# Residual gates of a two-layer diffusion backbone: rows spread over the partitions through a scratch in DRAM in place of a shuffle and GpSimd broadcasts

## The chip, the cores and the metric

The kernel runs on one core of one Trainium2 chip. The metric is the device time of one execution in microseconds, taken as the median of several runs. The core has five engines that run at the same time and meet through semaphores: TensorE (PE in the profile, with its weight loads as PEld), VectorE (DVE), ScalarE (ACT), GpSimd (POOL) and SyncE (SP). SP computes nothing here. It issues every DMA of this program, one after another, and stops at an instruction whose semaphore has not yet come, with all later DMAs behind it.

## The reference

One inference step of a transformer-like trunk: 2 layers over 128 context tokens and 256 latent tokens, 1024 features. The two groups share the weights and differ in the modulation, which is computed from a conditioning vector of each:

```
for l in range(DEPTH):
    sh1, sc1, g1, sh2, sc2, g2 = split(silu(c) @ w_mod[l] + b_mod[l], 6)
    h  = rmsnorm(x, norm1_g) * (1 + sc1) + sh1
    p  = h @ w_in                       # recurrence heads, attention heads
    o_r = gated linear recurrence, both directions (4 heads)
    o_a = attention with normalised q and k, rotary for latent tokens (8 heads)
    x  = x + g1 * (concat(o_r, o_a) @ w_out)
    h2 = rmsnorm(x, norm2_g) * (1 + sc2) + sh2
    x  = x + g2 * (relu(h2 @ w1) ** 2 @ w2)
y = rmsnorm(x, final_norm_g)
```

g1 and g2 are the residual gates. Each is a row of 1024 numbers for the context tokens and another for the latent tokens; all tokens of a group use the same row. The change touches only how these rows get to where the update of x reads them.

## The kernel before, in words

**Tiles.** The 384 tokens are three tiles of 128 tokens: tile 0 is the context, tiles 1 and 2 the latent tokens. `x[t]` holds 128 tokens on the partitions and 1024 features. Every product is made in three parts: each operand is split into a high part that TensorE takes at full rate (`hi`, made by an ACT cast, line 356) and the rest (`lo`, made by a DVE subtraction, line 364), and high by high, low by high and high by low are summed in PSUM.

**Weights.** All weights stream in from DRAM as units of up to 128 x 1024 numbers (512 KB), issued on SP by `load_chain` (line 348). A unit lands in one of four `raw` tiles. It leaves that tile when DVE has made its `lo` part, or, for the units of the modulation `w_mod` that are summed on DVE (`mod_acc`, lines 378 and 380), when DVE has made its four products with the two conditioning vectors. So SP mostly waits for a `raw` tile, and a load starts when DVE frees one. `hi` and `lo` have four tiles each, and parts of larger regions take more units in the MLP.

**The gates.** There are four: (layer 0, g1), (layer 0, g2), (layer 1, g1), (layer 1, g2), in the code `(l, ("g", 0))` and `(l, ("g", 1))`. The products of `w_mod` with the conditioning leave a gate in a PSUM bank as 4 x 256 numbers on partitions 0, 32, 64, 96 for the context and on partitions 1, 33, 65, 97 for the latent tokens. `mod_chain` then adds the bias on DVE (`brow`, line 442, into a `gev` tile), copies the latent rows from partitions 1, 33, ... to 0, 32, ... with a DVE shuffle (line 444), and spreads each of the eight pieces over all 128 partitions of `G` with eight GpSimd broadcasts (line 448). `G` is one tile of 128 x 2 x 1024 for all four gates, so a gate can be written only when the gate before it has been used up; the key `gfree` says so. The third gate waits for that at the end of layer 0.

**The update of x.** For each token tile and each half of the features, `xupd_chain` multiplies the PSUM bank of the products by `G` on DVE (line 638) and adds the result to x, the first half on POOL and the second on DVE (line 641).

**The norm.** `rms_steps` sums the squares of a tile on ACT (line 473), adds the two halves on DVE (line 475) and raises the sum to the power -1/2 on POOL (line 476, one column of 128 numbers). DVE scales x by that (line 487), TensorE transposes the scaled tile in eight pieces (line 492), ACT and DVE apply the modulation (lines 506, 504), and they split the result into `Hh` and `Hl` (lines 515, 516), which the next products read. The powers for the q, k and recurrence norms are made on POOL too (line 467).

**The end of a layer.** After the last products with w2 (line 1148) the three tiles get their update and their norm for the next layer one after the other, and the products with the q, k and v columns of w_in follow (`qk_part`, lines 568 and 569: six products for a unit of weights and a token tile; the first four units are taken for the tiles 0, 1 and 2 in turn, then the last four).

**The order of the work.** Nothing is left to the hardware: a class `Sched` holds some hundred chains of steps, each with an engine, an assumed duration, the keys it reads and writes and the tiles it takes and frees. It plays a rough model of the engines, and emits the step that could start first, with priorities; each engine then runs its list in order. A change of the assumed engine or duration of a step therefore moves other steps too.

Of the kernel before, what the change touches and what calls it, by code (L numbers as in the profile page):

```python
# [4 lines left out]
F32 = mybir.dt.float32  # L5
# [8 lines left out]
L = 2  # L14
# [11 lines left out]
class Sched:  # L26
    """Emits the steps of several chains in the order in which a rough model of the engines could start them."""

# [87 lines left out]
def c_dve(n, fast=False, extra=0):  # L116
    return 0.07 + n * (0.52e-3 if fast else 1.04e-3) + 0.06 * extra
# [10 lines left out]
def step_kernel(tc, A):  # L128
# [12 lines left out]
    def sb(name, shape, dt=F32):  # L141
        return P.tile(shape, dt, name=name, tag=name)
# [34 lines left out]
    sch.add_slots("hi", [sb(f"hi{i}", [128, 1024], F32R) for i in range(4)])  # L177
    sch.add_slots("lo", [sb(f"lo{i}", [128, 1024], F32R) for i in range(4)])
    regs = {}

# [84 lines left out]
    def warm_chain(nm, since, until, cold):  # L265
        """products of zeros that keep the tensor engine's clock up while its operands are on their way"""
        z = S0[:, 0, 0:2].rearrange("p h n -> p (h n)").bitcast(BF16)
        n = 0
        while until not in sch.t:
            yield S("PE", 0.44 if n < cold else 0.22, lambda: PE.matmul(get(nm), z[:, 0:128], z[:, 0:512], start=True, stop=True), r=since, acq=[("ps", nm)] if n == 0 else [], w=[nm])  # L270
            n += 1
        if n:
            yield S("PE", 0.0, lambda: None, rel=[nm])

# [1 line left out]
    units = []  # L276
# [50 lines left out]
    def split_prio():  # L327
        # units that are ready for the products and not used yet
        left = sum(1 for k in sch.bound if k[0] == "lo")
        return 0.5 if left <= 1 else 6  # L330
# [4 lines left out]
    def early_reg():  # L335
        """before the first layer's chains need them, the regions take the weights of its modulation"""
        def f():
            rs = [regs["xnT"][:, 3072:], region("B", "eB", F32), region("C", "eC", F32)]
            sch.add_slots("raw0", [r[:, i * 1024:(i + 1) * 1024] for r in rs for i in range(r.shape[1] // 1024)])
        yield S("POOL", 0.0, f, acq=[("rB", "eBr"), ("rC", "eCr")], r=["xnTreg"], w=["early"])  # L340
        yield S("POOL", 0.0, lambda: None, r=[("modps", 0, tag) for tag in mod_tags(0)[0]], rel=["eBr", "eCr"], w=["early_done"])
# [24 lines left out]

# [1 line left out]
    def mod_acc(l, tag):  # L368
# [15 lines left out]
    def mod_chain(l, tag):  # L384
# [7 lines left out]
        if (l, tag) in mod_dve:  # L392
            # the products with the two conditioning vectors on DVE, the sum over partitions on PE
            acc = {(i, h): ("modacc", l, tag, i, h) for i in range(2) for h in range(2)}

            def mm():
                for i in range(2):
                    for j in range(4):
                        m = 32 if i == 0 else 2
                        PE.matmul(get(nm)[32 * j:32 * j + m, 0:256], sel[:, 32 * i:32 * i + m], get(acc[i, j // 2])[:, (j % 2) * 256:(j % 2) * 256 + 256], start=i == 0, stop=i == 1, tile_position=(0, 32 * j))  # L400
            yield S("PE", 1.0, mm, r=[("modacck", l, tag, i, h) for i in range(2) for h in range(2)] + ["ini"], acq=[("ps", nm)], rel=list(acc.values()) + [("mtok", l, tag)], w=[nm])
        else:
            for u in us:
                def mm(u=u):
                    raw = get(("raw",) + u)
                    for i in range(kk):
                        k = u[3] + i
                        m = 32 if k == 0 else 2
                        for j in range(J):
                            o = (i * J + j) * N  # L410
                            PE.matmul(get(nm)[32 * j:32 * j + m, 0:N], cT[:, k, 0:m], raw[:, o:o + N], start=k == 0, stop=k == 7, tile_position=(0, 32 * j))  # L411
                yield S("PE", kk * (0.51 if N == 256 else 0.29), mm, r=[("rawk",) + u, "cT"], acq=[("ps", nm)] if u is us[0] else [], rel=[("raw",) + u],
                        w=[nm] if u is us[-1] else [], key=u)
# [26 lines left out]
        else:  # L440
            gi = tag[1]
            yield S("DVE", c_dve(256), lambda: V.tensor_tensor(out=get(ev)[:, 0:256], in0=get(nm)[:, 0:256], in1=brow[:, gi, :], op=ALU.add),
                    r=[nm, ("brow", l)], acq=[("gev", ev)], rel=[nm], w=[nm + (1,)])
            yield S("DVE", c_dve(256), lambda: V.stream_shuffle(out=get(ev)[:, 256:512], in_=get(ev)[:, 0:256], mask=[1] + [0] * 31), r=[nm + (1,)], w=[nm + (2,)])
            prev = [("gfree", l, gi)] if (l, gi) != (0, 0) else []

            def pb(i, j):
                return lambda: PO.partition_broadcast(G[:, i, j * 256:(j + 1) * 256], get(ev)[32 * j:32 * j + 1, i * 256:(i + 1) * 256])
            for i in range(2):
                for j in range(4):  # L450
                    last = i == 1 and j == 3
                    yield S("POOL", 0.45, pb(i, j), r=[nm + (2,)] + prev, rel=[ev] if last else [], w=[("gate", l, gi)] if last else [])

# [6 lines left out]

# [1 line left out]
    def rstd_steps(ss, n, inv, kin, kout):  # L462
# [6 lines left out]
    def rms_steps(nm, t, xi, ss):  # L469
        """w: nm + ("rs",); returns the column with (sum x^2 + D eps)^-1/2, to be multiplied by sqrt(D) = 32"""  # L470
        for hf in range(2):
# [62 lines left out]

# [1 line left out]
    def tok_unit(l, u, k0, kk, ncol, accs, first, last, extra_r=(), acq=()):  # L536
        """activation-stationary: accs[t][:, :ncol] += h[:, t].T @ w"""
        for t in range(NT):
# [64 lines left out]
    def wout_chain(l):  # L603
        accs = {(t, hf): ("acc", l, "wo", t, hf) for t in range(NT) for hf in range(2)}

        def step(j, t, hf, last):
            """the part j of the inner dimension: first the attention's, then the recurrence's"""
            g = j if j < 4 else j - 4
# [38 lines left out]

# [1 line left out]
    def rope_prep(l):  # L649
# [28 lines left out]
    def qk_chain(l, t):  # L678
# [10 lines left out]
        yield S("DVE", c_dve(512), lambda: V.tensor_reduce(out=ss[:, 0:8], in_=v3(get(nm + ("sq",)), 8), axis=AX.X, op=ALU.add), r=[nm + ("sq",)], rel=[nm + ("sq",)], w=[nm + ("ss",)])  # L689
        # the queries' factor holds the 1/8 of the scores  # L690
        yield from rstd_steps(ss, 10, ((slice(0, 8), 1.0, 64 * EPS), (slice(8, 10), 1.0 / 64, EPS)), nm + ("ss",), nm + ("rs",))
# [44 lines left out]
        if t == 0:  # L736
            yield S("ACT", c_act(512, True), lambda: ACT.copy(out=qTs[l], in_=v3(get(pq), 4)), r=[pq, ("tokreg", l)] + prev, rel=[pq], w=[("qk", l, t)])
            return
        # a tile's queries lie where its result of the attention will: in two parts for the products with the keys
        ts = slice(t * 128, (t + 1) * 128)  # L740
# [3 lines left out]
    def attn_region(l):  # L744
        # where the recurrence will keep its products and the projections their gates
        def f():
# [94 lines left out]

# [1 line left out]
    def hg_views(l, hp):  # L843
# [12 lines left out]
    def exps(l):  # L856
        """the exponentials of a layer's attention; the sigmoids follow, so that ACT changes its tables once"""
        return [("att", l, 0, kv, "p") for kv in range(2)] + [("att", l, t, g, 2) for t in (1, 2) for g in range(4)]
# [48 lines left out]
    def hg_levels(l, hp):  # L907
        # QQ: [backward, forward]; KK, TT: [forward, backward]; units of 128 columns: 2 heads x 3 chunks
        ini = [("hgi", l, 2 * hp), ("hgi", l, 2 * hp + 1)]
        AC = ACs[hp]  # L910

        def mm(m, nm):
            QQ, KK, TT, PR = hg_views(l, hp)
            ps = get(nm)
            for u in range(6):
                o = u * 128
                if m == 64:
                    for j in range(2):
                        # rows of half j against the columns of the other half: forward from j = 0, backward from j = 1
                        PE.matmul(ps[64 * j:64 * j + 64, u * 64:u * 64 + 64], PR[:, o + 64 * j:o + 64 * j + 64], QQ[:, (1 - j) * 768 + o + (1 - j) * 64:(1 - j) * 768 + o + (1 - j) * 64 + 64],  # L920
                                  start=True, stop=True, tile_position=(0, 64 * j))
                    continue
# [154 lines left out]

# [1 line left out]
    mreg = {}  # L1079
# [32 lines left out]
    def mlp_chain(l, tail=5):  # L1112
# [14 lines left out]
        def w1_last(p):  # L1127
            """the last token tile's part of a pair of hidden tiles: tokens on the partitions, so that the products are wide"""
            a = ("zt", l, p)
# [82 lines left out]

# [1 line left out]
    def tok_reg(l):  # L1214
# [14 lines left out]

# [1 line left out]
    def mod_units(l, tag):  # L1231
# [18 lines left out]
    def mix_in(us, mods, first=0, last=None):  # L1250
        """the units of the modulation's weights, spread over the others"""
        ms = []
# [154 lines left out]
```

## Time and profile before

| | us |
|---|---|
| median of 3 runs | 1012.4 |
| lowest and highest run | 1012.01, 1016.22 |
| span of the profiled execution | 1010.4 |
| PE busy | 981.0 |
| DVE busy | 685.1 |
| ACT busy | 495.5 |
| POOL busy | 70.9 |

For the profiled execution the page gives only its span, from the first to the last instruction; a time of its own from outside is not listed. The median of the timed runs is 2.0 us above that span.

How to read the rows: in the page's groups stands the line of the kernel, the engine, the operation, what is written and read, how many times, the busy time and the mean of one. A row of the timeline has the start and the length in us, the engine, the line, the operation, and in brackets for how long the engine was idle before and what ended that. A row of the waits has who waited for whom, the total in us, how many times, and the longest. A row of the chain of waits has the start, the length and what the time belongs to. A table by windows has a stretch of the span, the busy time and number of instructions of each engine in it, then the granted clock of TensorE (1.00 is full), the share of the DMA engines and GB/s.

### The profile page before, as it was taken

To read this page: it belongs to the slowest core of one execution; us is meant where nothing else is said; L and a number is where in the kernel's file an instruction comes from. 1 tells how busy PE (TensorE), PEld (TensorE's weight loads), DVE (VectorE), ACT (ScalarE), POOL (GpSimd) and SP (SyncE) were. 2 spreads that over 40 slices of the span, in tenths; PEclk is the share of its full clock that TensorE was granted. 3 is DMA by queue.
4 is the path that set the end of the run, shared out by engine and by line. 5 is a ranking of instruction groups with operands and counts; after the bars stand their busy time and mean duration, and the time that the engine had idled before them with its cause. 6 is when DMAs were issued, how large, how long until landed. Compare 5 with 4: busy or idle time off the path is not lost.

```text
span 1010.4 us, 17391 instructions
## 1 busy us (share of the span) xinstructions
PE 981.0 (97%) x6925; PEld 837.3 (83%) x6925; DVE 685.1 (68%) x1177; ACT 495.5 (49%) x903; POOL 70.9 (7%) x81
## 2 busy tenths in 40 slices
PE   8999999999999999999996999999999999999997
PEld 5785677889988879889885988888799999999895
DVE  3687676777898888888563787987765444434434
ACT  4356655545544443434352677755555444444432
POOL 0022000111020000000021200011110000000102
PEclk9999999999999999999997999999999999999999
DMA  9957555253577777776511432242435544444411
GB/s 314 313 165 225 186 173 187 74 168 98 184 236 241 229 235 221 222 246 207 181 40 52 134 104 83 85 116 76 129 120 188 168 144 147 146 146 146 146 42 62
DMA packets 140017, 161.17 MB, mean 160 GB/s; under 512 B 5776, under 2 KB 105488, under 8 KB 139936
## 3 DMA queue, kind: packets, MB, share of 16 engines
q1 hardware_dynamic: 139936, 160.06, 51.3%
q8 instruction: 54, 0.88, 0.3%
q14 instruction: 27, 0.22, 0.1%
HBM read 157.16 MB, written 2.88 MB: 158 GB/s over the span
## 4 chain that ended last, share of the span: by engine, by line
PE 80%; DMA 10%; DVE 5%; issue 2%; ACT 1%; POOL 1%; SPq 0%; POOLq 0%; DVEq 0%; ACTq 0%
PE bank L1122 21%; PE bank L1148 21%; PE bank L587 9%; DMA raw<-w_mod_d 7%; PE bank L546 6%; PE bank L618 6%; PE bank L568 3%; DVE t L380 3%; PE bank L411 1%; PE bank L934 1%; PE bank L569 1%; PE bank L835 1%; PE bank L1137 1%; DVE lo L364 1%; PE bank L789 1%
## 5 line engine op out<-in xcount | busy, mean ns | idle before, releaser
L356 ACT CAST hi<-raw 128x1024 fp32r<-128x1024 f32 (+1 forms) x152 | 155.5, 1028 | 121.7 <-DMA raw<-w_d 42.0
L364 DVE TENSOR_TENSOR lo<-raw,hi 128x1024 fp32r<-128x1024 f32 (+1 forms) x152 | 180.5, 1195 | 43.8 <-ACT hi L356 43.3
L380 DVE SCALAR_TENSOR_TENSOR t<-raw,cT,t 128x512 f32<-128x512 f32 x196 | 135.7, 749 | 32.1 <-DMA raw<-w_mod_d 31.8
L1122 PE MATMUL bank<-mA,hi 128*128 128x384 f32 (+1 forms) x336 | 111.8, 333 | 0.0
L1122 PE MATMUL bank<-mA,lo 128*128 128x384 f32 (+1 forms) x336 | 111.1, 331 | 0.0
L1122 PE MATMUL bank<-mB,hi 128*128 128x384 f32 (+1 forms) x336 | 110.9, 330 | 0.0
L1107 ACT ACTIVATE t<-bank 128x384 f32<-128x384 f32 x64 | 31.4, 491 | 145.2 <-PE bank L1122 145.0
L1110 DVE TENSOR_TENSOR mB<-t,mA 128x384 fp32r<-128x384 f32 x64 | 35.8, 559 | 95.2 <-ACT mA L1109 95.1
L1148 PE MATMUL bank<-lo,mA 128*128 128x512 f32 x252 | 98.8, 392 | 0.0
L1148 PE MATMUL bank<-hi,mB 128*128 128x512 f32 x252 | 98.7, 392 | 0.0
L1148 PE MATMUL bank<-hi,mA 128*128 128x512 f32 x252 | 98.0, 389 | 0.0
L1122 PE MATMUL bank<-mA,wts 128*128 128x384 f32 (+1 forms) x352 | 89.0, 327 | 0.0
L1148 PE MATMUL bank<-wts,mA 128*128 128x512 f32 x264 | 87.8, 393 | 0.0
L356 ACT CAST wts<-raw 128x1024 fp32r<-128x1024 f32 x44 | 46.2, 1050 | 56.1 <-DMA raw<-w_d 28.8
L587 PE MATMUL bank<-Hh,hi 128*128 128x384 f32 x192 | 69.4, 362 | 0.6 <-ACT hg L864 0.6
L364 DVE TENSOR_TENSOR wts<-raw,wts 128x1024 fp32r<-128x1024 f32 x44 | 54.5, 1241 | 21.0 <-ACT wts L356 21.0
L1122 PEld LDWEIGHTS bank<-mA,hi 128*128 128x128 f32 x336 | 63.2, 188 | 2.6 <-issue 0.9
L587 PE MATMUL bank<-Hh,lo 128*128 128x384 f32 x192 | 64.6, 337 | 0.0
L587 PE MATMUL bank<-Hl,hi 128*128 128x384 f32 x192 | 64.5, 336 | 0.0
L1122 PEld LDWEIGHTS bank<-mB,hi 128*128 128x128 f32 x336 | 63.2, 188 | 1.3
L1122 PEld LDWEIGHTS bank<-mA,wts 128*128 128x128 f32 x352 | 62.5, 188 | 1.7 <-issue 0.9
L1122 PEld LDWEIGHTS bank<-mA,lo 128*128 128x128 f32 x336 | 63.2, 188 | 0.0
(255 smaller groups left out, 1981.3 us busy)
## 6 DMA issues: line engine op xcount, KB each, us to landing
raw<-w_d SPq DMA_DIRECT2D x128, 512.0 KB, 4.2
raw<-w_mod_d SPq DMA_DIRECT2D x80, 512.0 KB, 4.4
raw<-w_in_d SPq DMA_DIRECT2D x40, 512.0 KB, 4.9
raw<-w_in_d SPq DMA_DIRECT2D x16, 384.0 KB, 4.1
raw<-w_out_d SPq DMA_DIRECT2D x16, 256.0 KB, 4.1
raw<-w_out_d SPq DMA_DIRECT2D x8, 512.0 KB, 3.6
eB<-w_mod_d SPq DMA_DIRECT2D x12, 256.0 KB, 6.4
eC<-w_mod_d SPq DMA_DIRECT2D x8, 256.0 KB, 6.2
```

The lines of the kernel that those rows point to most:

```text
L356: yield S("ACT", c_act(n), lambda u=u, n=n: ACT.copy(out=get(("hi",) + u)[:, 0:n], in_=get(("raw",) + u)[:, 0:n]), r=[("rawk",) + u] + ([( ...
L364: yield S("DVE", c_dve(n), lambda u=u, n=n: V.tensor_tensor(out=get(("lo",) + u)[:, 0:n], in0=get(("raw",) + u)[:, 0:n], in1=get(("hi",) + ...
L380: V.scalar_tensor_tensor(out=o, in0=raw, scalar=c, in1=o, op0=ALU.mult, op1=ALU.add)
L411: PE.matmul(get(nm)[32 * j:32 * j + m, 0:N], cT[:, k, 0:m], raw[:, o:o + N], start=k == 0, stop=k == 7, tile_position=(0, 32 * j))
L546: PE.matmul(ps, a, b, start=(first and k == 0 and i == 0), stop=(last and k == kk - 1 and i == 2))
L568: PE.matmul(get(aq), a, b[:, 0:512], start=st and i == 0, stop=sp and i == 2)
L587: PE.matmul(ps, a, b, start=(k == 0 and i == 0), stop=(k == 7 and i == 2))
L618: PE.matmul(ps, a, b, start=j == 0 and i == 0, stop=j == 7 and i == 2)
L1107: yield S("ACT", c_act(384, True), lambda: ACT.activation(out=get(r_)[:, 0:384], in_=get(z)[:, 0:384], func=AF.Relu), r=[z], acq=[("t2", r ...
L1110: yield S("DVE", c_dve(384), lambda: V.tensor_tensor(out=get(u)[1], in0=get(t_)[:, 0:384], in1=get(u)[0].bitcast(F32), op=ALU.subtract), r ...
L1122: PE.matmul(get(z)[:, cs], a, b, start=(k == 0 and i == 0), stop=(k == 7 and i == 2))
L1148: PE.matmul(get(("acc", l, "w2", t, hf)), a, b, start=(f == 0 and i == 0), stop=(f == NF - 1 and i == 2))
```

## The change

The shuffle and the eight broadcasts of each gate are replaced by DMAs on SP. For each gate there is a scratch tensor in DRAM of 2 x 4 x 256 numbers. Two small DMAs write the rows of `gev` from the partitions 0, 32, 64, 96 and 1, 33, 65, 97 to it (4 x 1 KB each). A third DMA reads the 8 KB back and writes them to each of the 128 partitions of `G`, 1 MB in all. The scheduler is told that the first step takes 0.8 us and the second 3.0 us of SP. The `gev` tile is freed after the first step, and the next layer's load of `brow` (line 457), whose key is that of the removed shuffle, now follows the write to the scratch.

```diff
@@ step_kernel
+    PD = pool("dr", bass.MemoryType.DRAM)
+    gate_rows = {(l, gi): PD.tile([2, 4, 256], F32, name=f"grow{l}{gi}", tag=f"grow{l}{gi}") for l in range(L) for gi in range(2)}
...
@@ mod_chain
             gi = tag[1]
             yield S("DVE", c_dve(256), lambda: V.tensor_tensor(out=get(ev)[:, 0:256], in0=get(nm)[:, 0:256], in1=brow[:, gi, :], op=ALU.add),
                     r=[nm, ("brow", l)], acq=[("gev", ev)], rel=[nm], w=[nm + (1,)])
-            yield S("DVE", c_dve(256), lambda: V.stream_shuffle(out=get(ev)[:, 256:512], in_=get(ev)[:, 0:256], mask=[1] + [0] * 31), r=[nm + (1,)], w=[nm + (2,)])
             prev = [("gfree", l, gi)] if (l, gi) != (0, 0) else []
-
-            def pb(i, j):
-                return lambda: PO.partition_broadcast(G[:, i, j * 256:(j + 1) * 256], get(ev)[32 * j:32 * j + 1, i * 256:(i + 1) * 256])
-            for i in range(2):
-                for j in range(4):
-                    last = i == 1 and j == 3
-                    yield S("POOL", 0.45, pb(i, j), r=[nm + (2,)] + prev, rel=[ev] if last else [], w=[("gate", l, gi)] if last else [])
+            gd = gate_rows[l, gi]
+
+            def put():
+                for i in range(2):
+                    SP.dma_start(out=gd[i], in_=get(ev)[i:128:32, 0:256])
+            yield S("SP", 0.8, put, r=[nm + (1,)], rel=[ev], w=[nm + (2,)])
+            yield S("SP", 3.0, lambda: SP.dma_start(out=G.rearrange("p i n -> p (i n)"), in_=gd.rearrange("i j n -> (i j n)").partition_broadcast(128)),
+                    r=[nm + (2,)] + prev, w=[("gate", l, gi)])
```

The rest of the diff drops comments. Two lines are added near the top of `step_kernel`, so most lines of the changed kernel have a number that is 2 higher (638 becomes 640, 476 becomes 478).

The scheduler makes a new order out of this. Three places of it matter below.

**First place: the end of layer 0, on POOL.** `sm` holds the sums of squares, `pw` the exponent, the `x` tiles the three token tiles, `t` tiles are scratch. A row named ISA without operands sets up GpSimd for another kind of operation. Before:

```order
L641 TENSOR_TENSOR x_92<-x_92,t_4_111 128x512
L476 TENSOR_TENSOR sm<-sm,pw 128x1
L641 TENSOR_TENSOR x_93<-x_93,t_0_107 128x512
L476 TENSOR_TENSOR sm<-sm,pw 128x1
L641 TENSOR_TENSOR x_94<-x_94,t_0_107 128x512
L448 ISA
L448 ISA G<-gev_127 128x256 x8
L476 ISA
L476 TENSOR_TENSOR sm<-sm,pw 128x1
```

Now:

```order
L643 TENSOR_TENSOR x_92<-x_92,t_4_111 128x512
L478 TENSOR_TENSOR sm<-sm,pw 128x1
L643 TENSOR_TENSOR x_93<-x_93,t_1_108 128x512
L478 TENSOR_TENSOR sm<-sm,pw 128x1
L643 TENSOR_TENSOR x_94<-x_94,t_1_108 128x512
L478 TENSOR_TENSOR sm<-sm,pw 128x1
```

The eight broadcasts of the third gate and the two set-ups stood between the update of the third tile and the power of its norm; now the power follows the update. On the whole, POOL has no broadcast left, and no set-up but the first.

**Second place: SP at the second gate (layer 0, g2), amid the MLP weights `w_d` and the modulation `w_mod_d`.** Before:

```order
L348 DMA raw_118<-w_d 128x1024
L348 DMA raw_116<-w_mod_d 128x2x512
L457 DMA brow<-brow_d 4x512 x2
L348 DMA raw_115<-w_d 128x8x128
L348 DMA raw_117<-w_mod_d 128x2x512
```

Now:

```order
L350 DMA raw_118<-w_d 128x1024
L350 DMA raw_116<-w_mod_d 128x2x512
L451 DMA grow_130<-gev_134 4x256 x2
L350 DMA raw_115<-w_d 128x8x128
L453 DMA G<-grow_130 128x2048
L459 DMA brow<-brow_d 4x512 x2
L350 DMA raw_117<-w_mod_d 128x2x512
```

Two writes and the copy to `G` are new; the load of `brow` moves behind the copy, and the next `w_mod` unit stands behind all of them. At the first and the fourth gate it is much the same, with two and one weight loads between the writes and the copy. At the third gate the writes stand in the MLP of layer 0, and the copy far behind them, between the sixth and the seventh of the eight q, k, v units of layer 1.

**Third place: TensorE at the start of layer 1, the products of q (568, now 570) and of k and v (569, now 571) and the transposes of the third tile (492, now 494).** `hi_119` to `hi_122` are the first four units; the bank tells the token tile (before: 65 and 66 the first, 67 and 61 the second; now: 67 and 68 the first, 63 and 61 the second). Before:

```order
L568 MATMUL bank_67<-hi_120,Hl 128x512
L569 MATMUL bank_61<-hi_120,Hl 128x256
L568 MATMUL bank_67<-lo_124,Hh 128x512
L569 MATMUL bank_61<-lo_124,Hh 128x256
L492 MATMUL bank_64<-cst,t_5_112 128x128 x4
L492 MATMUL bank_68<-cst,t_2_109 128x128 x4
L568 MATMUL bank_67<-hi_121,Hh 128x512
```

Now:

```order
L570 MATMUL bank_67<-lo_126,Hh 128x512
L571 MATMUL bank_68<-lo_126,Hh 128x256
L494 MATMUL bank_65<-cst,t_0_107 128x128 x4
L494 MATMUL bank_66<-cst,t_3_110 128x128 x4
L570 MATMUL bank_63<-hi_119,Hh 128x512
```

The transposes stood behind two of the second tile's four units; now they stand ahead of all four.

## The prediction

> **What bounds the kernel now.** I read the page's totals and slices first.
>
> ```profile
> span 1010.4 us, 17391 instructions
> PE 981.0 (97%) x6925; PEld 837.3 (83%) x6925; DVE 685.1 (68%) x1177; ACT 495.5 (49%) x903; POOL 70.9 (7%) x81
> PE   8999999999999999999996999999999999999997
> GB/s 314 313 165 225 186 173 187 74 168 98 184 236 241 229 235 221 222 246 207 181 40 52 134 104 83 85 116 76 129 120 188 168 144 147 146 146 146 146 42 62
> ```
>
> TensorE is busy for 97% of the span. Taking work from DVE and POOL is worth nothing where PE never waits for it. But one slice in the middle, the 22nd (530 to 556 us), has PE at 6 tenths, and DMA is nearly silent there. So I looked for PE's longest waits, and for who made its releaser late.
>
> ```profile
> PE bank L492 <- DVE t L487: 10.3, 2, 9.8
> DVE t L487 <- POOL sm L476: 19.3, 12, 12.1
> ```
>
> One wait of 9.8 us stands out: transposes wait for DVE's scaled tile, and that waited 12.1 us for a power on POOL. The chain of waits at this place, which is the end of layer 0:
>
> ```profile
> 531.69 1.25 issue
> 532.94 3.44 POOL G L448 x8
> 536.45 6.73 issue
> 543.18 0.60 POOL sm L476
> 543.80 0.50 DVE t L487
> ```
>
> The broadcasts of the third gate are in the chain, though that gate is first read in the attention's update of layer 1, behind all its q, k, v products. The timelines of POOL and DVE tell how:
>
> ```profile
> 514.72 0.60 POOL L476 TENSOR_TENSOR sm<-sm,pw 128x1 f32<-128x1 f32 x1 [3.74 <-DVE sm L475]
> 524.78 1.94 POOL L641 TENSOR_TENSOR x<-x,t 128x512 f32<-128x512 f32 x1 [1.60 <-DVE t L638]
> 532.94 3.44 POOL L448 PARTITION_BROADCAST G<-gev  x8 [6.23 <-issue]
> 543.18 0.59 POOL L476 TENSOR_TENSOR sm<-sm,pw 128x1 f32<-128x1 f32 x1 [6.80 <-issue]
> 530.61 0.21 DVE L475 TENSOR_SCALAR sm<-sm 128x1 f32<-128x1 f32 x1
> 530.74 0.95 DVE L364 TENSOR_TENSOR lo<-raw,hi 128x768 fp32r<-128x768 f32 x1
> ```
>
> POOL ended the third tile's update at 526.72, was silent for 6.23 us, broadcast for 3.44, was silent again for 6.80, and only then made a power whose input was there at 530.82. The two silences have no releaser; they stand where POOL changes its kind of work. After the first tile, whose power follows an update directly, the same step started 0.09 us after its input (514.42 + 0.21 = 514.63, start 514.72).
>
> **What the stall costs.** TensorE around it:
>
> ```profile
> 524.43 1.04 PE L492 MATMUL bank<-cst,t 128*128 128x128 f32 x8
> 525.23 0.48 PE L1148 MATMUL bank<-wts,mA 128*128 128x512 f32 x1
> 527.38 0.39 PE L568 MATMUL bank<-hi,Hh 128*128 128x512 f32 x1
> 530.74 0.50 PE L568 MATMUL bank<-lo,Hh 128*128 128x512 f32 x1 [0.39 <-DVE lo L364]
> 544.35 1.97 PE L492 MATMUL bank<-cst,t 128*128 128x128 f32 x8 [9.81 <-DVE t L487]
> 545.97 0.78 PE L568 MATMUL bank<-hi,Hh 128*128 128x512 f32 x1
> 549.91 0.40 PE L568 MATMUL bank<-hi,Hh 128*128 128x512 f32 x1
> 550.96 0.39 PE L568 MATMUL bank<-hi,Hh 128*128 128x512 f32 x1
> 546.00:548.00 2.00, 2.00 (x8) 1.71 (x7) 1.64 (x5) 1.87 (x5) 0.00 (x0) 0.50 0.00 0
> 550.00:552.00 2.00, 2.00 (x14) 1.75 (x13) 0.32 (x1) 0.99 (x2) 0.00 (x0) 1.00 0.00 0
> ```
>
> Two terms. The wait itself is 9.81 us. And behind it the granted clock is 0.50, until the products are at 0.40 us again from 549.91 on: eight transposes take 545.97 - 544.35 = 1.62 us where the second tile's took 525.23 - 524.43 = 0.80, and two units of six products take 549.91 - 545.97 = 3.94 where one unit at full clock takes 550.96 - 549.91 = 1.05. That is 0.82 + 1.84 = 2.66 us more.
>
> Now I build the same stretch for the changed kernel, up to the same point: all products of the first two tiles with the first four units, and the third tile's transposes, are done. Before that is 549.91. After: from 527.38, four units for the first tile, 4 x 1.05 + the wait of 0.39 = 4.59, to 531.97. The transposes stand here now. The power starts 0.09 after 530.82 and takes 0.60, to 531.51; DVE ends its split at 531.69 and scales two halves of 0.44 each (0.88 for two in this trace), to 532.57. So PE waits some 0.2 us for the first half and 0.4 for the second, and has the eight transposes done at about 533.0. Four units for the second tile end at 537.2. The gain is 549.91 - 537.2 = **12.7 us**. The third tile's Hh and Hl follow the transposes as before, by 537, covered by the second tile's 4.2 us. Everything after, to the end of the span, hangs on TensorE, busy nearly without a gap, and moves forward with it.
>
> Of the clock: after 9.81 us without work the next product of 512 columns takes 0.78, after 0.39 us only 0.50. [...]
>
> **What the change removes elsewhere.** The other three gates:
>
> ```profile
> 86.68 5.65 POOL L448 PARTITION_BROADCAST G<-gev  x8 [24.60 <-DVE gev L442]
> 291.56 6.14 POOL L448 PARTITION_BROADCAST G<-gev  x8 [44.48 <-DVE gev L442]
> 938.31 4.36 POOL L448 PARTITION_BROADCAST G<-gev  x8 [199.49 <-DVE gev L442]
> L638 DVE TENSOR_TENSOR t<-bank,G x24: 682/691/692, 221.3 to 1003.0; 128x512 f32<-128x512 f32 x24
> ```
>
> The first gate is spread at 86.68 and first read at 221.3. The second is spread as the MLP of layer 0 begins and read at its end; the fourth is spread at 938.31, and its reads end the program at 1003. POOL has nothing urgent behind any of these. Their removal is 0, and so is that of the four shuffles, which DVE makes right behind its additions and nobody on PE's path reads. The same distances hide the latency of the new DMAs as such; what they can cost is time for others, on SP's queue and on the DMA engines.
>
> **What the change adds.** Per gate, SP issues two small writes and a copy of 1 MB. At the second gate the timeline of SP has:
>
> ```profile
> 291.53 1.12 SPq L457 DMA_DIRECT2D brow<-brow_d  x2
> 295.16 0.38 SPq L348 DMA_DIRECT2D raw<-w_d  x1
> 296.53 0.37 SPq L348 DMA_DIRECT2D raw<-w_mod_d  x1
> 301.23 2.08 DVE L380 SCALAR_TENSOR_TENSOR t<-raw,cT,t 128x512 f32<-128x512 f32 x3 [0.67 <-DMA raw<-w_mod_d]
> new_v_d<-vS SPq DMA_DIRECT2D x2, 64.0 KB, 3.4
> ```
>
> The two writes take the place of `brow` at 291.53, and SP has them out by 292.65. The slowest write to DRAM in this trace lands after 3.4 us, so the rows are there at 296.0. The unit of 295.16 starts as before, since it waits for a tile. The copy then starts at 296.0, SP takes 0.4, `brow` another 1.1, and the `w_mod` unit starts at 297.6 instead of 296.53: 1.1 us late, and behind 1.05 MB that take 3.3 us at the 314 GB/s of the first slice. It lands up to 4.4 us late, and DVE already waits for this one at 301.23. That is the worst case for the second gate. The best is 0: `hi` and `lo` tiles lie ahead of PE, DVE is rid of its shuffle, and PE hardly waits for DVE's sums here:
>
> ```profile
> PE bank L400 <- DVE t L380: 1.2, 3, 0.5
> PE bank L411 <- DMA raw<-w_mod_d: 4.2, 7, 1.6
> ```
>
> (the first row for 250 to 420 us, the second for the whole span). I take 1.0, near the lower end, because a delay must first use up what is loaded ahead. The first gate stands among `w_mod` units that PE does wait for, in seven small waits: again 0 to 4.4, and I take 0.5. At the third gate the writes stand late in that MLP, where PE's slices are at 9 up to the 21st: 0. Its copy stands between the sixth and seventh q, k, v unit.
>
> ```profile
> 530.71 1.36 SPq L348 DMA_DIRECT2D raw<-w_in_d  x2
> raw<-w_in_d SPq DMA_DIRECT2D x16, 384.0 KB, 4.1
> ```
>
> These are the seventh and the eighth, which wait for DVE's splits. The copy has its rows since long and waits only for the last read of `G`, ahead of those splits on DVE. It delays the seventh by at most its 3.3 us, to 530.71 + 4.1 + 3.3 = 538.1, and its turn comes when the third tile's third unit frees a split tile, at 537.2 + 3 x 1.05 = 540.4: 0, with 2.3 us to spare. The fourth gate stands where PE's slices are at 9: 0.
>
> The order moves in three stretches (88 to 160, 290 to 410, and the boundary). I give that 1.5 us to either side, from the size of PE's single gaps (up to 1.6 in the row above).
>
> **Sum.** -12.7 + 1.0 + 0.5 = -11.2 us, on the span 1010.4: 999.2. The median of the runs lies 2.0 above that span, and I keep that: **1001.2 us**. Its own range is 998.2 (no cost, order 1.5 better) to 1005.6 (half of both upper bounds, order 1.5 worse).
>
> **Rivals.**
> - *Same gain, dear loads.* Both the first and second gate pay their 4.4 us in full: -12.7 + 8.8 = -3.9, 1008.5. For it: DVE's wait at 301.23 has no slack in it. Against it: the tiles ahead of PE, and PE's sums of waits.
> - *The stall moves into loads.* The copy of the third gate makes the seventh and eighth unit late beyond 540.4, say because it runs at half the rate I took: 3.3 more, less 2.3 of slack, 1.0 us; with as much again for the eighth, about 1003.2.
> - *POOL still pauses.* If the silence of 6.80 us belongs to the power itself, part of the stall stays: a gap of near 6.8, gain 12.7 - 6.8 = 5.9 or less, 1006.5. Against it: 514.72, where a power follows an update at once.
> - *Slower.* SP must wait for the scratch rows to land before it issues the copy, with all weights behind it. If rows queue behind loads in flight, landing takes not 3.4 but up to 10 us, and each of the first two gates costs up to 4.4 + 6.6 = 11.0. From 6.4 us each on, the change loses; at 9 each it ends at 1012.4 - 12.7 + 18 = 1017.7. Against it: at 291 to 296 the loads ahead are two, and small writes in this trace land within 3.4.
>
> [...]
>
> **Chances.** The forecast 0.72, dear loads 0.15, moved into loads 0.04, POOL still pauses 0.04, slower 0.05. A measurement of this kernel can tell about 0.5% (5.1 us) from no change. Faster by more: 0.72 + 0.07 (half of dear loads) + 0.04 + 0.03 = 0.86; within: 0.08 + 0.01 = 0.09; slower: 0.05. The range to hold the time 8 times in 10: 998.0 to 1007.0.
>
> **What would show it.** Right: no set-up and no broadcast on POOL; the third tile's power within 0.2 us of its DVE input; PE's longest wait near that point under 1 us; granted clock 1.00 from 530 to 560; the end of layer 0 to the first attention product of layer 1 shorter by some 12 us. The costs: SP's waits for the scratch and DVE's waits for `w_mod` near 86 and 291, and PE's waits at 400 and 411 (402 and 413 now). Wrong: a PE gap of several us at the same transposes, or PE waits in 88 to 160 or 290 to 410 that grow by more than 5 us.

## The result, and the profile after

The changed kernel takes 999.59 us (median of 4 runs, 999.38 to 1002.09) where the kernel before, beside it on the same chip, takes 1012.2 (4 runs, 1011.61 to 1016.22): a ratio of 0.9882, with a 95% interval of 0.9861 to 0.9904. Run twice more beside the experiments it gave 0.9896 (0.9879 to 0.9913) and 0.9905 (0.9888 to 0.9922). So it is about 1.1% faster, and the forecast of 1001.2 lies 1.6 us beside the measured median. That it lies so near is in part luck. The span of the profiled execution came out at 1000.3 where 999.2 was forecast. But that execution was the slowest of the four (1002.09), so the median lies 0.7 us below the span and not 2.0 above it. Against the kernel before, the forecast was 11.2 us less; the three medians are 12.6, 10.8 and 10.6 us less.

The page of the changed kernel, totals and TensorE's slices:

```profile
span 1000.3 us, 17353 instructions
PE 980.1 (98%) x6925; PEld 836.4 (84%) x6925; DVE 680.7 (68%) x1169; ACT 495.6 (50%) x903; POOL 51.9 (5%) x49
PE   8999999999999999999999999999999999999997
```

The slice that stood at 6 is at 9. PE's busy time has hardly moved (981.0 before), the span has lost 10.1 us: nearly all of what went was waiting. Two of PE's waits over the whole span (us in total, times, longest), the largest sum and the one at the transposes:

```profile
PE bank L413 <- DMA raw<-w_mod_d: 4.6, 5, 2.0
PE bank L494 <- DVE t L489: 0.7, 2, 0.5
```

The wait of 9.8 us at the transposes (now line 494) is gone. The place itself, in the timelines of POOL, DVE and PE (start, duration, engine):

```profile
526.79 1.88 POOL L643 TENSOR_TENSOR x<-x,t 128x512 f32<-128x512 f32 x1 [1.66 <-DVE t L640]
532.82 1.20 POOL L478 TENSOR_TENSOR sm<-sm,pw 128x1 f32<-128x1 f32 x1 [4.15 <-DVE sm L477]
532.52 0.21 DVE L477 TENSOR_SCALAR sm<-sm 128x1 f32<-128x1 f32 x1
532.65 0.95 DVE L366 TENSOR_TENSOR lo<-raw,hi 128x768 fp32r<-128x768 f32 x1
534.05 0.88 DVE L489 TENSOR_SCALAR t<-x,sm 128x512 f32<-128x512 f32 x2 [0.44 <-POOL sm L478]
529.29 0.39 PE L570 MATMUL bank<-hi,Hh 128*128 128x512 f32 x1
534.59 1.09 PE L494 MATMUL bank<-cst,t 128*128 128x128 f32 x8 [0.27 <-DVE t L489]
539.76 0.40 PE L570 MATMUL bank<-hi,Hh 128*128 128x512 f32 x1
```

POOL stands without work between the third tile's update and its power, and starts the power 0.09 us after its input (532.52 + 0.21 = 532.73). PE waits 0.27 us. From the first q, k, v product (529.29) to the end of four units for two tiles with the transposes between (539.76) are 10.47 us; the same work took 549.91 - 527.38 = 22.53 before. That is **12.06 us** less. The clock (the column behind POOL's) is whole there:

```profile
530.00:545.00 15.00, 14.34 (x84) 12.07 (x83) 10.30 (x18) 8.49 (x15) 1.20 (x1) 1.00 0.41 147
545.00:570.00 25.00, 25.00 (x155) 22.98 (x154) 17.58 (x42) 14.87 (x38) 6.98 (x3) 1.00 0.51 139
```

To see whether anything else moved, I cut both executions at the first update that POOL makes in each of the four updates of the residual stream. Before:

```profile
222.05 1.29 POOL L641 TENSOR_TENSOR x<-x,t 128x512 f32<-128x512 f32 x1 [11.62 <-DVE t L638]
509.69 1.29 POOL L641 TENSOR_TENSOR x<-x,t 128x512 f32<-128x512 f32 x1 [211.99 <-DVE t L638]
713.27 1.29 POOL L641 TENSOR_TENSOR x<-x,t 128x512 f32<-128x512 f32 x1 [11.60 <-DVE t L638]
986.91 1.29 POOL L641 TENSOR_TENSOR x<-x,t 128x512 f32<-128x512 f32 x1 [44.24 <-DVE t L638]
```

After:

```profile
224.19 1.30 POOL L643 TENSOR_TENSOR x<-x,t 128x512 f32<-128x512 f32 x1 [11.59 <-DVE t L640]
511.56 1.29 POOL L643 TENSOR_TENSOR x<-x,t 128x512 f32<-128x512 f32 x1 [262.37 <-DVE t L640]
703.49 1.29 POOL L643 TENSOR_TENSOR x<-x,t 128x512 f32<-128x512 f32 x1 [11.68 <-DVE t L640]
977.05 1.28 POOL L643 TENSOR_TENSOR x<-x,t 128x512 f32<-128x512 f32 x1 [248.06 <-DVE t L640]
```

Call the four stretches A (start to layer 0's attention update; the first gate is spread in it), B (to layer 0's MLP update; the second gate), C (to layer 1's attention update; the third gate's old place) and D (to layer 1's MLP update; the fourth gate). Before and after they take 222.05 and 224.19, 287.64 and 287.37, 203.58 and 191.93, 273.64 and 273.56. C gives 11.65 us; A gives 2.1 back; B and D change by 0.3 us and less. The same cuts serve for all kernels below.

### The profile page after: what moved, and what is told of

The parts are those of the page before. It is cut to its first block, busy times and chain, and to the rows that moved or that the text cites. A ratio compares the mean times of both kernels' runs of the same rounds, so it can differ in the third digit from the quotient of the medians.

```text
span 1000.3 us, 17353 instructions
## 1 busy us (share of the span) xinstructions
PE 980.1 (98%) x6925; PEld 836.4 (84%) x6925; DVE 680.7 (68%) x1169; ACT 495.6 (50%) x903; POOL 51.9 (5%) x49
## 4 chain that ended last, share of the span: by engine, by line
PE 76%; DMA 11%; DVE 7%; issue 2%; ACT 2%; SPq 0%; POOL 0%; POOLq 0%; DVEq 0%; ACTq 0%
PE bank L1124 19%; PE bank L1150 19%; PE bank L589 9%; DMA raw<-w_mod_d 8%; PE bank L548 6%; PE bank L620 6%; DVE t L382 4%; PE bank L570 3%; PE bank L413 2%; PE bank L936 1%; PE bank L571 1%; DVE lo L366 1%; PE bank L1139 1%; PE bank L837 1%; DMA raw<-w_in_d 1%
```

## The experiments

Theory S (the stall) says that the whole gain is what stood on POOL between the third tile's update and its power: two silences and eight broadcasts. Theory R (relief) says that the gain comes from taking shuffles and broadcasts off DVE and POOL elsewhere, and from the new order of the work. A second question is what the DMAs cost at the first two gates. Each kernel ran beside the kernel before. The ratios are to it, with 95% intervals (its median was 1012.2 beside the first run of the change and 1013.5 to 1014.4 beside the others, so medians of different groups of runs are not to be compared); A to C are of the profiled execution, in us.

| kernel | median us | ratio | A | B | C |
|---|---|---|---|---|---|
| before (profile shown above) | 1012.2 | 1 | 222.05 | 287.64 | 203.58 |
| the change | 999.59 | 0.9882 (0.9861 to 0.9904) | 224.19 | 287.37 | 191.93 |
| third gate alone by DMA | 1004.21 | 0.9898 (0.9875 to 0.9921) | 227.48 | 287.45 | 191.78 |
| all but the third by DMA | 1012.71 | 0.9976 (0.9961 to 0.9990) | 224.66 | 286.99 | 203.51 |
| no DMA, power ahead of broadcasts | 1007.61 | 0.9928 (0.9907 to 0.9948) | 222.75 | 288.45 | 197.60 |
| no broadcasts of the third gate | 1002.15 | 0.9877 (0.9853 to 0.9901) | 223.54 | 289.22 | 191.60 |
| no DMA, broadcasts late | 1001.43 | 0.9879 (0.9859 to 0.9899) | 223.58 | 289.09 | 191.77 |
| the change, first two gates left out | 999.97 | 0.9865 (0.9846 to 0.9884) | 222.30 | 288.58 | 191.95 |
| the change, first two copies twice | 1013.94 | 1.0013 (0.9997 to 1.0028) | 229.79 | 294.73 | 191.89 |
| the change, copies late | 1003.47 | 0.9906 (0.9889 to 0.9923) | 223.94 | 289.79 | 191.91 |
| all by DMA, in the old order | 1007.81 | 0.9952 (0.9937 to 0.9968) | 228.92 | 290.56 | 191.67 |
| first gate by broadcasts, the rest by DMA | 1002.47 | 0.9888 (0.9870 to 0.9906) | 224.53 | 288.04 | 191.93 |
| the change, second time | 1002.96 | 0.9896 (0.9879 to 0.9913) | 224.82 | 287.48 | 191.96 |
| the change, third time | 1002.94 | 0.9905 (0.9888 to 0.9922) | 226.00 | 288.46 | 191.98 |

C repeats within 0.4 us wherever the stall is gone. A does not. Five kernels have the same instructions there: before, the power ahead, no third broadcasts and broadcasts late take 222.05 to 223.58, but the third gate alone takes 227.48. The change takes 224.19 to 226.00 in its three executions. So a difference of 2 us in A, read from one execution each, is not yet a price.

### Is it the third gate?

Only the third gate by DMA, and all but the third:

```
-            yield S("DVE", ..., stream_shuffle ...)      # and eight broadcasts
+            if (l, gi) == (1, 0):                        # the other kernel: != (1, 0)
+                (the two writes and the copy of the change)
+            else:
+                (shuffle and broadcasts as before)
```

> Only the third gate goes by DMA; the other three keep shuffle and broadcasts. Theory S (the stall: the whole gain is what POOL's two silences and eight broadcasts put between the third tile's update and its power at the end of layer 0): 12.0 us of 1012.2 gone, 1000.2, with PE's longest wait near 535 below 1 us; if the DMAs of the first and second gate cost the 1.5 us that were predicted, it is 1.5 faster than the change, near 998. Theory R (the gain comes from the other gates, that is from DVE's shuffles and POOL's broadcasts taken away beside the weights' splits, and from the new order of the work there): within 2 us of the kernel before, 1010 to 1014.

> The first, second and fourth gate go by DMA; the third keeps shuffle and broadcasts. Theory S: the wait of 9.8 us and the half clock behind it stay, so 1012.2 plus what the DMAs of the first two gates cost, 0 to 2 us: 1012 to 1014.5. Theory R: nearly the whole gain, 1000 to 1003.

Third alone: 0.9898, C 191.78. All but the third: 0.9976, C 203.51. Theory S has it. The median of third alone is 10.2 us below that of the kernel before beside it, not 12.0. In its profiled execution A is long: the clock there was at half from 20.6 to 27.4 us, about a wait of 2.05 us and long before any gate; what its other executions lost is not known. The second half of the first expectation failed: this kernel is not 1.5 us faster than the change, so it shows no price for the DMAs of the first two gates. All but the third still shows the stall whole, in its waits and on POOL:

```profile
PE bank L505 <- DVE t L500: 11.1, 2, 10.0
534.37 3.44 POOL L461 PARTITION_BROADCAST G<-gev  x8 [5.61 <-DVE lo L366]
545.42 0.59 POOL L489 TENSOR_TENSOR sm<-sm,pw 128x1 f32<-128x1 f32 x1 [7.62 <-issue]
```

It is 0.24% faster than the kernel before, where Theory S expected 0 to 2 us slower. So the three other gates may be worth some 2.4 us together, DMAs and order included, and no more of Theory R stays; where these would lie, the profiled execution doesn't show (A and B together 511.65, in the kernel before 509.69).

### Is it the broadcasts, or where they stand?

Three kernels without any DMA. In the first the third gate's broadcasts also wait for the third tile's power; TensorE, VectorE, ScalarE and SyncE keep the order of the kernel before, but for the third tile's eight transposes on TensorE, which stand ahead of the second tile's units as in the change.

```
             prev = [("gfree", l, gi)] if (l, gi) != (0, 0) else []
+            if (l, gi) == (1, 0):
+                prev.append(("nrm", 1, 0, 2, "rs"))
```

> No DMA at all: the kernel before, in which the third gate's broadcasts also wait for the third tile's power, so POOL makes the power first. Theory S: the power follows its input at once, 1000 +- 1.5, although POOL still broadcasts all four gates; its silences and broadcasts, 6.2 + 3.4 + 6.8 = 16.4 us, then end near 550 (in the time of the changed kernel), just where POOL's next work, the first power of layer 1's queries, is due at 550.45; if they end later, each us there is one more. Theory R: 1010 to 1012, since every broadcast and shuffle is still there.

It came out at 0.9928, and C at 197.60: half of the gain. POOL and PE show where the other half went:

```profile
532.39 1.19 POOL L478 TENSOR_TENSOR sm<-sm,pw 128x1 f32<-128x1 f32 x1 [4.18 <-DVE sm L477]
539.95 6.22 POOL L450 PARTITION_BROADCAST G<-gev  x8 [6.36 <-issue]
555.58 2.00 POOL L469 TENSOR_TENSOR sm<-sm,pw 128x10 f32<-128x10 f32 x1 [9.42 <-issue]
558.76 0.47 PE L732 MATMUL bank<-cst,t 128*128 128x128 f32 x1 [4.42 <-DVE t L702]
```

The power is made at once and the transposes wait no longer. But silence, broadcasts and silence take 6.36 + 6.22 + 9.42 = 22.0 us here, not the 16.4 that I had added up from the kernel before, and the next power, that of layer 1's first queries, comes 5.6 us after its input. PE waits 4.42 us for it, and the clock is at half for 3.41 us there. The stall moved to the next place where POOL changes its kind of work. The expectation had named this limit ("each us there is one more"), but 1000 +- 1.5 was a miss.

In the second the broadcasts wait still longer, until POOL has made the three 128x10 powers:

```
+            if (l, gi) == (1, 0):
+                prev += [("qkn", 1, t, "rs") for t in range(NT)]
```

> No DMA: the kernel before, in which the third gate's broadcasts wait until POOL has made the three 128x10 powers of layer 1's queries; POOL has nothing to do from 567 to 657 us, and the gate is read at 703. Theory S, as the earlier run with the power ahead of the broadcasts left it (the set-ups cost wherever a due power stands behind them): no stall at all, neither at 535 nor at 555, ratio 0.988 as for the kernel without the third gate's broadcasts (0.9877). If broadcasts cost by themselves (what they take from DVE or from the loads), 0.990 to 0.993.

0.9879, C 191.77. POOL pauses ahead of the broadcasts as before; a pause behind them would lie within the 79.28 us in which nobody needs POOL:

```profile
574.43 5.08 POOL L450 PARTITION_BROADCAST G<-gev  x8 [6.02 <-issue]
658.80 0.74 POOL L469 TENSOR_TENSOR sm<-sm,pw 128x2 f32<-128x2 f32 x1 [79.28 <-DVE sm L467]
```

One line, no scratch, no DMA, and as fast as the change: beside it the change has 0.9896, and the intervals overlap. In the third the third gate's broadcasts are left out:

```
             def pb(i, j):
+                if (l, gi) == (1, 0):
+                    return lambda: None
```

> The kernel before without the third gate's eight broadcasts, every other instruction in its old order (layer 1's attention update reads the second gate's rows, so this is the price of the broadcasts and no version). Theory S: the built sum of the stall alone, 12.7 us: 999.5, or 1000.2 by the 12.0 us seen between the two traces at the boundary. Theory R: at most 2 us faster than before, 1010 or more. The clock at 535 to 560 is full by S.

0.9877, C 191.60, with every other instruction in its old order, the transposes behind two units of the second tile too: so their new place is worth nothing that C shows. This is the price of the stall by itself, 12.0 us in C. Together the three show that it was not the broadcasting wherever it stands, nor DVE's shuffles, but the broadcasts with a silence on either side ahead of a due power. In the kernel before these three take 6.23 + 3.44 + 6.80 us, so the silences are 13.0 of some 16.5.

### What do the DMAs cost?

First the changed kernel with the writes and the copies of the first two gates left out, then with each of these copies issued twice, the order of all else kept. In the first, one more VectorE instruction, not shown here, fills `G` with zeros at the start:

```
             def put():
+                if l == 0:
+                    return
```
```
+                for n in range(2 if l == 0 else 1):
                     SP.dma_start(out=G..., in_=gd...partition_broadcast(128))
```

> The changed kernel without the two writes and the copy of the first and of the second gate, all else in its order (layer 0 reads a G of zeros; this prices those DMAs). If they cost the 1.5 us that were predicted (0.5 and 1.0): 1.5 faster than the changed kernel, ratio to the kernel before 0.9867 where the change has 0.9882; if they cost nothing on TensorE's path, 0.9882. The dear-loads rival (4.4 each) has 8.8 us here, ratio 0.980.

> The changed kernel with the 1 MB copy of the first and of the second gate issued twice, all else in its order. Each second copy delays the loads behind it by another 3.3 us or so. If the prediction's 1.5 us are right and grow with the delay: 2 to 4 us slower than the changed kernel, ratio 0.990 to 0.992; if the loads ahead hide the copy with room to spare, 0.988 to 0.989; dear loads: 6 or more us slower, 0.994 and up.

> The changed kernel as it is, beside the others on the same chip: ratio 0.988.

Side by side: none 0.9865, one 0.9896, two 1.0013. From none to one are 3.1 us by the middle values, give or take 2.6 (the half intervals 0.0019 and 0.0017, added in squares, of 1013.7): the predicted 1.5 lies inside, zero just outside, and the 8.8 of dear loads far outside. At the `w_mod` products of line 413 (414 where the DMAs are left out), from 88 to 160 us, PE waits 2.2 us in the one execution without these DMAs, and 3.3, 4.1 and 4.6 in the three of the change; that goes the same way, but single executions scatter as much (below). From one copy to two are 11.9 us, far more than the 2 to 4 expected; that is where the expectation had put dear loads (6 or more). SP's wait and PE's, in the kernel with two:

```profile
SPq L455 <- DMA G<-grow: 6.8, 1, 6.8
102.88 1.08 PE L413 MATMUL bank<-raw,cT 128*32 128x256 f32 x8 [4.38 <-DMA raw<-w_mod_d]
331.82 1.01 PE L1127 MATMUL bank<-mA,wts 128*128 128x384 f32 x2 [2.59 <-DVE wts L366]
```

The second copy writes the same tile, so SP holds it (and every load behind it) for 6.8 us until the first has landed; this run doubles the bytes and adds a block of the queue, and can't part the two. It shows that the cover of the copies is thin: 6.8 us more at the first gate make PE wait 4.38 us for `w_mod`, and the clock is at half for 6.83 us there. A grows by 5, B by 7.

Next, all four gates by DMA, planned with the durations of the old steps, so that PE and ScalarE keep the order of the kernel before word for word:

```
-            yield S("SP", 0.8, put, ...)
-            yield S("SP", 3.0, copy, ...)
+            yield S("DVE", c_dve(256), put, ...)
+            for n in range(8):
+                yield S("POOL", 0.45, copy if n == 0 else lambda: None, ...)
```

> All four gates by DMA, but planned with the old steps' durations, so that TensorE, ScalarE and VectorE keep the order of the kernel before (VectorE less its four shuffles). If the new order of the work is worth nothing: as the changed kernel, 0.988 to 0.990, and the stretch from the first update of layer 0's MLP to the first update of layer 1's attention 191.6 to 192.0 us. The prediction gave the order 1.5 us to either side: 0.9867 to 0.991. Theory R would have 0.995 or more, since the new order is gone.

> The changed kernel as it is, beside the three others on the same chip: ratio 0.988 to 0.990.

0.9952 against 0.9905 of the change beside it: 4.8 us slower than the change, outside what I had allowed for the order. C is 191.67, so the stall is not the reason; A is 228.92 and B 290.56. The rows of PE at the two places, and of SP at the first:

```profile
101.17 1.08 PE L413 MATMUL bank<-raw,cT 128*32 128x256 f32 x8 [3.24 <-DMA raw<-w_mod_d]
337.04 1.20 PE L402 MATMUL bank<-t,sel 128*32 128x256 f32 x8 [2.63 <-DVE t L382]
90.02 0.34 SPq L454 DMA_DIRECT2D G<-grow  x1
91.65 17.12 SPq L350 DMA_DIRECT2D raw<-w_mod_d  x3
```

The copy of the first gate goes out at 90.02, the next `w_mod` load comes behind it, and PE in the old order is at its product at 97.93 (101.17 - 3.24): 3.24 us too early. In the kernel before, without the copy, the same product starts at 97.30 and waits for nothing:

```profile
97.30 0.64 PE L411 MATMUL bank<-raw,cT 128*32 128x256 f32 x8
```

PE's waits for `w_mod` loads from 88 to 160 us add up to 6.6 us here, and to 1.9 to 4.3 in the five kernels that have the old order there and none of these DMAs. In the changed kernel the same stretch of PE:

```profile
97.50 0.88 PE L791 MATMUL bank<-cst,tok 128*128 128x128 f32 x6
98.77 0.34 PE L769 MATMUL bank<-kTl,mAh 64*128 64x384 f32 x2
99.55 0.64 PE L413 MATMUL bank<-raw,cT 128*32 128x256 f32 x8 [0.44 <-issue]
```

The planner, which holds SP for 3.0 us for the copy, has put more of attention's work ahead of the `w_mod` product, and PE waits only 0.44 us. So the DMAs are not cheap at these places. In the old order they cost some 7.5 us (0.9952 against 0.9877 and 0.9879 of the two kernels above that have the old order, no DMA and no stall), in the new order 3.1: the new order hides the larger part of them.

Last, two ways to make them cheaper: the first two copies issued later, where loads are few, and the first gate back on broadcasts:

```
+            if l == 0:    # behind the last w_mod load, or the last w_d load, of layer 0
+                late = [("rawk",) + ...]
-                    r=[nm + (2,)] + prev, ...
+                    r=[nm + (2,)] + prev + late, ...
```

> The changed kernel, but the copy of the first gate is issued after the last w_mod load of layer 0's attention part (near 152 us instead of 89; it is read at 211), and that of the second behind the last w_d loads of layer 0 (near 493 instead of 298; read at 509); the order of the work is planned anew by that. If the two copies cost 1.5 to 3 us where they stand (as the run without them and the run with them twice point to), these come back: ratio 0.985 to 0.987 where the changed kernel has 0.9882 to 0.9896. If they cost nothing there: 0.988 to 0.990. If the second lands after 509, the update waits and it is slower than the changed kernel.

> The first gate by shuffle and broadcasts, the other three by DMA. Prices the first gate's DMAs: if they cost 0.5 us as predicted, within 1 us of the changed kernel; if 2 us, as the offset between the two traces at 222 had it, ratio 0.986 to 0.987.

0.9906 and 0.9888 beside the change's 0.9905. Neither can be told from it. If 1.5 to 3 us are to be had at the first two gates, these two kernels don't fetch them: the planner orders the work anew each time, and A and B change by 1 to 2 us with the order. No kernel of this study beats the change beyond its interval.

## Why the prediction was right

- **What bounds the kernel.** Right: C alone carries the gain, and the kernel without the third gate's broadcasts has all of it. That the broadcasts of a gate that is needed 180 us later stood in the chain of waits was the reading that counted.
- **The term of -12.7.** 12.06 measured in the stretch it was built for. What was mis-sized is the power: 0.60 taken, 1.20 measured, where it starts 0.17 us behind DVE's split at 532.65 (below). By that the scaling of the third tile starts 4.76 us after the first q product (529.29 to 534.05) where 4.31 was built (527.38 to 531.69), 0.45 of the 0.64 us that are missing. The wait before the transposes is 0.27 where 0.2 was built; the clock stayed at 1.00. The sum takes the full clock behind its waits of 0.2 and 0.4 us; the record of the granted clock has 1.00 there, in the kernel before from 530 to 539 us with the wait of 0.39 us in it, and in the change from 530 to 570 us with the 0.27. By C it is 11.65, so another 0.4 us was given back before 703, nearly all of it behind this stretch (703.49 - 539.76 = 163.73, before 713.27 - 549.91 = 163.36); what gave it back was not traced.
- **Third gate's copy at 0, with 2.3 us to spare.** Right: it went out at 530.56, the seventh and eighth unit at 532.63 and 533.67, and PE has no gap there. The fourth gate at 0: D is 273.56 against 273.64. Right.
- **First and second gate, 0.5 and 1.0.** The sum is not contradicted (the run without them: 3.1 us, give or take 2.6, for both), but the reason was wrong. I had it that tiles loaded ahead of PE hide the copies. In the old order the same DMAs make A 5 to 7 us and B 1 to 3 us longer than in the kernels with that order and no DMA there (the third gate alone, with its half clock early in A, left aside): that is the rival "dear loads", with a price near what it had (4.4 each). What hides most of it is the order.
- **Order, 1.5 us to either side.** This is the step that was wrong, although the time came out within the range. I treated the moved rows as noise of the size of PE's single gaps, apart from the price of the DMAs. With the DMAs, planned anew or not is worth 4.8 us, because the order decides whether PE comes to a `w_mod` product before or after the delayed load (3.24 us of wait in the old order, 0.44 us in the new, at the one near 100 us). Without the DMAs of the first two gates the two orders can't be told apart (0.9865 anew, 0.9879 old, overlapping intervals).
- **"POOL still pauses".** Refuted: the power follows its input after 0.09 us. The pause stood only where broadcasts come before (6.80, 7.62 and 9.42 us in three kernels).
- **"Slower".** Its mechanism is there, at a small price; a landing as late as 10 us, which it set as its worst case, shows at neither of the first two gates, in the change or in the old-order kernel. SP at the second gate, and its wait for the scratch (us in total, times, longest):

```profile
293.93 1.08 SPq L451 DMA_DIRECT2D grow<-gev  x2
298.52 0.34 SPq L453 DMA_DIRECT2D G<-grow  x1
SPq L453 <- DMA grow<-gev: 1.7, 1, 1.7
```

SP stood 1.7 us there (2.7 in the old order), with the loads behind it; the copy goes out 3.5 us after the second write's issue ended (293.93 + 1.08 = 295.01). That is the 3.4 I took from the slowest write. At the first gate of the old-order kernel it was 1.7 us (87.23 + 1.07 = 88.30 to 90.02), so the 3.4 holds for one of the two and not for the other.

## What to carry to other kernels

Look at what a slow switch of an engine's kind of work (here POOL's, 5.6 to 6.4 us before the broadcasts and 6.8 to 9.4 us before the next power) stands in front of. A job that nobody needs soon can hold up one that is due, and here it was enough to move the job to where the engine is idle for longer than both switches (79.28 us behind the broadcasts). When such a job is moved to DMA, part of its price is the loads that queue behind it (in the old order PE waited 3.24 us for one of them). Here most of that was hidden only in the order that was planned with the DMAs' time; a run in the old order is what showed it. A gain that repeats within 0.4 us in its own stretch can be read there when the whole program scatters by several us.

## What the runs showed of the hardware

- **POOL's switch is paid both ways and is not constant.** Before a group of broadcasts: 5.61 (the profile names a DVE split as its end), 6.02, 6.23 and 6.36 us; before the first power after it: 6.80, 7.62 and 9.42. Why they differ, and what POOL does in them, no run here shows.
- **A power that starts during a VectorE instruction took longer.** 0.55 to 0.60 us with nothing beside it, 1.19 to 1.20 in the ten kernels whose third power at the end of layer 0 comes at its turn, 0.16 to 0.17 us behind the start of a 128x768 split (the change and all others but the kernel before and all but the third). In the change the split runs to 533.60 and the power ends at 534.02, 0.42 us behind it. Beside a shorter one in the kernel before, a VectorE product of line 378 (128x512, 246.19 to 246.67), the power from 246.35 took 0.72 us, to 247.07: 0.40 us behind the product's end. Whether the power waited for the instruction or ran more slowly beside it, no run here separates.
- **Half clock came in pieces of 3.41 us, and a short wait brought one.** The traces' record of the granted clock shows 0.50 for 10.24 us at the wait of 9.81, for 6.83 at 4.38, 3.24 and 2.05, and for 3.41 at 4.42, 2.59, 1.97 and 1.72, each beginning within the wait or up to 1.9 us behind it. One of the shorter ones, with a table by windows:

```profile
146.61 0.61 PE L413 MATMUL bank<-raw,cT 128*2 128x256 f32 x8 [1.97 <-DMA raw<-w_mod_d]
126.00:150.00 24.00, 21.93 (x334) 18.60 (x333) 17.48 (x36) 11.58 (x17) 0.00 (x0) 0.94 0.55 179
150.00:160.00 10.00, 10.00 (x72) 6.81 (x71) 2.63 (x8) 4.92 (x10) 0.00 (x0) 0.96 0.81 262
```

Waits at the same product of 1.55 us in the kernel before and of 1.63 us in the one with broadcasts late brought none, nor did the 2.63 us at 337 in the old order. The 1.97 us that brought one are shorter than the piece itself. So equal instructions lost a piece in one execution and not in the next, which is a part of the scatter in A: the third gate alone has 6.83 us of half clock there, the change's first and third execution 3.41 each. It is not all of it: the change's second execution has no such piece in A and is no shorter there (224.82).
